# Low parts of the mLSTM query and key weights and tiles on VectorE instead of GpSimd, in a two-layer encoder on one core

## The chip, the cores and the metric

One core of a Trainium2 chip runs the whole program. The metric is the device time of one execution in microseconds. TensorE (PE in the rows) multiplies, VectorE (DVE) and ScalarE (ACT) do the element-wise work, GpSimd (POOL) does some of it, and SyncE (SP) issues most of the loads from HBM.

## The reference

Two encoder layers of 512 tokens and 1024 channels. Each has a token mixer and a channel mixer. The mixer runs two branches on one modulated input u: a bidirectional mLSTM with four heads of 256 channels, and a dilated attention with three patterns. What the change touches are the mLSTM's query and key:

```python
qk = silu(centred_dwconv(u @ w_in[:, :2048], conv_w, conv_b))   # five taps along the tokens
q, k = split(qk, 2)                # 4 heads of 256 channels each
# per head, both directions:
s   = einsum('thd,shd->ts', q, k) * exp(log_d - m)
num = s @ v
h   = num / max(|den|, exp(-m))
y_a = (sigmoid(o) * norm(h) * gn_w) @ w_a
```

Everything is float32.

## The kernel before

**Products in three parts.** Each float32 operand is split in a high part (ScalarE casts it to fp32r, L87) and a low part (operand minus high part, L88, `split`). `mm3` (L90 to L93) issues three matmuls for one product: high by high (L91), then for `product` high weights by the low part of u (L92), then the low weights by the high part of u (L93). So TensorE asks for a tile's low weights only with the third matmul. `split` takes the engine of the subtraction as an argument; VectorE is the default.

**Weights.** `w_feature` (L116 on) loads 256 columns of weights (1 MB) through SP into one of two raw buffers, and gives them out in two halves of 128x1024, each with its high and low part in one of two pairs of buffers. A pair is free again when the product that read it two halves ago is done. The name `wqk` stands in `POOL`, so for query and key weights the subtraction runs on GpSimd; all other weights have it on VectorE.

**A head.** `head_qk` (L1068 to L1087) runs twice for a head, for query and for key, with two halves each: four products of 24 matmuls of 512 columns. Behind each product ScalarE copies the PSUM tile into `zp` (L1077) and makes the first tap (L1079), VectorE adds four taps (L1081, `cy`), ScalarE takes the tanh (L1082), VectorE finishes SiLU (L1083), ScalarE casts the high part `qkh` (L87), and the low part `qkl` is a subtraction of 128x512 (L1085, L88). `GQ = (0, 1)` holds both values of `n % 2`, so all of these run on GpSimd. `zp` and `cy` have two buffers.

After the four products `head_v` (L1089 on) makes the values: its first two PSUM tiles (`mv`) are the same two buffers that the query and key products use (tag `g`), so it can't begin before ScalarE has copied the third and fourth product into `zp`. `head_o` makes the output gate.

**Order.** The heads run in a pipeline: `head_scores` of one head (products `smx`, exponentials `dt`, and the split `pt`), then `weave` alternates the four products, values and gate of the next head with `head_out` of this one (`num`, the denominators `dn` in L1187 to L1201 with one power on GpSimd in L1200, `htp`). The first head's query runs inside the last attention step. Outside blocks under manual schedule, the framework's planner sets each engine's order from its own estimates; each engine then runs its list in order. In the first layer, accumulations of the next modulation (`acc`, L283) run on VectorE between all this, with their loads (`aw`) in SP's queue.

Of the kernel before, what the change touches and what calls it, by code (L numbers as in the profile page):

```python
# [35 lines left out]
NM = 8  # L36
AV = 'gS'
GORD = (0, 1, 2)
GQ = (0, 1)
MV = 'gA'  # L40
SD = ((0, 0, 0.5, 1, 1.5, 3, 3.5, 4, 4.5, 5, 5), (1, 1.5, 2, 2, 2.5, 4, 5.5, 6, 6.5, 7, 7))
SF = ((0, 0, 0.5, 1, 2, 3, 3), (1.5, 2.5, 3.5, 4, 5, 6, 6))
# [5 lines left out]
ENG = {mybir.EngineType.PE, mybir.EngineType.DVE, mybir.EngineType.Activation, mybir.EngineType.Pool}  # L48
OW = ((0, 2), (1, 0), (1, 2))
BG = 1  # L50
POOL = ("wqk",)
WV = (1, 1)
HO = ((0, 0), (0, 1), (1, 0), (0, 2), (1, 1), (0, 3), (1, 2), (1, 3))
Q = 18
# [11 lines left out]
def encoder(ctx: ExitStack, tc: tile.TileContext, a, depth):  # L66
    nc = tc.nc
    alpha = 4 ** 0.25
    V, S, G, Y = nc.vector, nc.scalar, nc.gpsimd, nc.sync
# [13 lines left out]
    def raw_tile(name):  # L83
        return wpool.tile([P, 2048], F32, tag="raw", name=name, bufs=RAW)

    def split(hi, lo, src, eng=None):
        S.copy(hi, src)  # L87
        (eng or V).tensor_tensor(lo, src, hi.bitcast(F32), op=ALU.subtract)  # L88
# [24 lines left out]
    def w_pair(name, off, k, n):  # L113

        return [wpool.tile([P, 1024 + WPAD], F32R, tag=t, name=name + t[1])[:, off:off + k * n]
                .rearrange("p (k n) -> p k n", n=n) for t in ("wh", "wl")]  # L116

    def w_feature(src, ktiles, name, own=None, count=2, eng=None):


        n = src.shape[1]
        cols = 2048 // ktiles
        srcv = src.rearrange("(k p) n -> p k n", p=P)
        for c0 in range(0, n, cols):
            cw = min(cols, n - c0)
            raw = raw_tile(name)
            rv = raw[:, :ktiles * cw].rearrange("p (k n) -> p k n", k=ktiles)
            Y.dma_start(rv, srcv[:, :, c0:c0 + cw])
            for j in range(cw // P):
                r = rv[:, :, j * P:(j + 1) * P]  # L130
                if own is not None and c0 // P + j < count:
                    yield split_own(r, ktiles, own, eng)
                    continue
                wh, wl = w_pair(name, 0, ktiles, P)
                split(wh, wl, r, G if name in POOL else V)
                yield [wh[:, k, :] for k in range(ktiles)], [wl[:, k, :] for k in range(ktiles)]

    def split_own(r, ktiles, own, eng):

        out = [], []  # L140
        for k in range(0, ktiles, 4):
            wh, wl = own(), own()
            split(wh[:], wl[:], r[:, k:k + 4, :], eng)
            for o, w in zip(out, (wh, wl)):
                o.extend(w[:, i, :] for i in range(4))
        return out
# [497 lines left out]
    with ExitStack() as st:  # L644
# [76 lines left out]
        with tc.manual_schedule(engines=ENG):  # L721
            for f in range(KT):
                wh, wl, _ = wq
# [11 lines left out]
    for l in range(depth):  # L735
# [13 lines left out]
        def slot(name, dt=F32):  # L749
            return X.tile([P, T], dt, tag="q", name=name, bufs=Q)  # L750
# [5 lines left out]
        def wk(name, shape=(P, T)):  # L756
            r = roles[name]
            return YP.tile(list(shape), F32, tag=r, name=name, bufs=depths[r])
# [57 lines left out]
        def att_qk(sp, given=None):  # L816

            q, k = {}, {}
            for g in GORD:
                c0 = COL_A + g * 512 + sp * P  # L820
                if given and given[g]:
                    ps = given[g]
                else:
                    ps = yield from gemm_steps(next(w_feature(w_in[:, c0:c0 + P], KT, "waq")), uk, KT, "aq")
                src = ps[:].rearrange("p (a i r) -> p a r i", a=4, r=4)
                if g:
                    q[g] = slot(f"q{g}")
                    S.activation(q[g][:].rearrange("p (a r i) -> p a r i", a=4, r=4), src, AF.Copy,
                                 scale=qsc[:, sp:sp + 1])
                    continue  # L830

                t = slot("q0")
                S.activation(t[:].rearrange("p (a r i) -> p a r i", a=4, r=4), src, AF.Copy, scale=qsc[:, sp:sp + 1])
                q[0] = [YP.tile([P, T + d], F32R, tag=n, name="qs", bufs=2) for n, d in (("cy", 0), ("zp", 4))]
                for s in range(2):
                    own, oth = slice(64 * s, 64 * s + 64), slice(64 - 64 * s, 128 - 64 * s)
                    S.copy(q[0][s][own, 0:T], t[own, :])
                    V.tensor_tensor(q[0][s][oth, 0:T], t[own, :], q[0][s][own, 0:T].bitcast(F32), op=ALU.subtract)
            for g in GORD:
                c0 = COL_A + 1536 + g * 512 + sp * P  # L840
                if given and given[3 + g]:
                    ps = given[3 + g]
                else:
                    w = first_k.pop(g, None) if given else None
                    ps = yield from gemm_steps(w or next(w_feature(w_in[:, c0:c0 + P], KT, "wak")), uk, KT, "ak")
                if g:
                    k[g] = slot(f"k{g}")
                    S.copy(k[g][:].rearrange("p (r j) -> p r j", r=4), ps[:].rearrange("p (j r) -> p r j", r=4))
                    continue

                kk = [slot(f"kk{s}", F32R) for s in range(2)]
                kl = YP.tile([P, T], F32R, tag="xd", name="kl", bufs=XD_)
                for s in range(2):
                    own, oth = slice(64 * s, 64 * s + 64), slice(64 - 64 * s, 128 - 64 * s)
                    S.copy(kk[s][own, :], ps[own, :])
                    S.copy(kk[s][oth, :], ps[own, :])
                    V.tensor_tensor(kl[own, :], ps[own, :], kk[s][own, :].bitcast(F32), op=ALU.subtract)
                k[0] = kk, kl
# [203 lines left out]
        def product(w, name, fine):  # L1062

            if fine:
                return (yield from gemm_steps(w, uk, KT, name))
            return gemm_f(w, uk, KT, name)

        def head_qk(h, sec, out, fine=False):  # L1068

            src = w_in[:, sec * COL_K + h * 256:sec * COL_K + h * 256 + 256]  # L1070
            for d, w in enumerate(w_feature(src, KT, "wqk")):
                n = sec * 8 + 2 * h + d
                ps = yield from product(w, "qk", fine)
                zp = wk("zp", (P, T + 4))
                G.memset(zp[:, 0:2], 0.0)
                G.memset(zp[:, T + 2:T + 4], 0.0)
                S.copy(zp[:, 2:T + 2], ps[:])  # L1077
                y = wk("cy")
                S.activation(y[:], zp[:, 0:T], AF.Identity, bias=vec["convb"](n), scale=vec["conv"](0, n))  # L1079
                for j in range(1, 5):  # L1080
                    V.scalar_tensor_tensor(y[:], zp[:, j:j + T], vec["conv"](j, n), y[:], op0=ALU.mult, op1=ALU.add)  # L1081
                S.activation(zp[:, 0:T], y[:], AF.Tanh, scale=0.5)  # L1082
                V.scalar_tensor_tensor(y[:], zp[:, 0:T], 1.0, y[:], op0=ALU.add, op1=ALU.mult)  # L1083
                th, tl = slot("qkh", F32R), slot("qkl", F32R)
                split(th[:], tl[:], y[:], G if n % 2 in GQ else V)  # L1085
                out.append((th, tl))
                yield  # L1087

# [31 lines left out]
        def head_lead(out):  # L1120

            o, qk = [], []
            yield from head_o(0, o, True)
            yield from head_qk(0, 0, qk, True)
            out.extend((o[0], qk))

        def head_gemm(h, out, begun=()):

            so, qk = begun or ([], [])
            vs, o = [], [so]  # L1130
            if not begun:
                yield from head_qk(h, 0, qk)
            yield from head_qk(h, 1, qk)
            yield from head_v(h, vs)
            if not begun:
                o = []
                yield from head_o(h, o)
            out.extend((qk, *vs, o[0]))
# [127 lines left out]
        for h in range(MH):  # L1266
            for d in range(2):
                th, tl = (PW.tile([P, T], F32R, tag="hgw", name=n, bufs=16) for n in ("hgh", "hgl"))
# [7 lines left out]
        for i in range(KT):  # L1276
# [6 lines left out]
            th = Z.tile([P, T], F32R, name=f"mh{i}")  # L1283
            tl = Z.tile([P, T], F32R, name=f"ml{i}")
# [35 lines left out]
        for i in range(FT):  # L1320
# [17 lines left out]
            th, tl = (F.tile([P, T], F32R, tag="f", name=n, bufs=2 * FT) for n in ("fh", "fl"))  # L1338
# [90 lines left out]
```

## Time and profile before

| what | before |
|---|---|
| time, median of three runs | 2257.79 us (2257.42 to 2259.61) |
| the profiled execution's own time | 2259.71 us |
| span of the profiled execution | 2257.9 us |
| busy: PE, DVE, ACT, POOL | 97%, 58%, 39%, 10% |
| heads of the first layer | about 325 to 570 us of the span |
| heads of the second layer | about 1430 to 1680 us of the span |

The profile is read in this order: the busy shares, then the same by stretch, then what TensorE waited for in the stretches that the change touches, then the groups of instructions there, and last the order of time inside one head. A matmul's row shows its pipelined duration, so consecutive matmuls overlap; idle time and its releaser stand in brackets.

### The profile page before, as it was taken

What the parts mean: (1) busy time and instruction counts of PE and PEld (TensorE: products, weight loads), DVE (VectorE), ACT (ScalarE), POOL (GpSimd) and SP (SyncE); (2) the same over time, 40 slices, a digit from 0 to 9 for tenths busy, and PEclk for the clock granted to TensorE, in tenths of its full rate; (3) what the DMA queues carried; (4) which work ended last, traced back from release to release, by engine and by line L of the source; (5) the groups of instructions that cost most, each with busy time, mean ns of one, the idle gap of its engine ahead of it and who ended that gap; (6) DMA issues with size and microseconds to landing.
All of it is one profiled execution on the core that took longest, in us unless ns stands there. A gap on an engine that the chain in (4) does not pass through costs nothing.

```text
span 2257.9 us, 30948 instructions
## 1 busy us (share of the span) xinstructions
PE 2189.0 (97%) x12353; PEld 1831.3 (81%) x12353; DVE 1307.3 (58%) x2290; ACT 883.7 (39%) x1465; POOL 220.0 (10%) x270
## 2 busy tenths in 40 slices
PE   6999999989999999999999999999999999999998
PEld 5877877878888888888888787788888888888886
DVE  8645348778664766664564544577764455533346
ACT  4544345544333522222364443455543334222222
POOL 4100003322000000000000000233300000000001
PEclk8999999999999999999999999999999999999999
DMA  9623223232343566654543233121212344422324
GB/s 242 188 84 108 85 80 103 75 102 81 106 146 105 196 211 200 202 193 165 184 162 103 62 97 101 57 68 64 75 57 93 103 171 147 163 93 94 112 102 158
DMA packets 244063, 278.78 MB, mean 123 GB/s; under 512 B 10280, under 2 KB 191184, under 8 KB 243920
## 3 DMA queue, kind: packets, MB, share of 16 engines
q1 hardware_dynamic: 238848, 258.97, 35.6%
q0 software_dynamic: 3584, 12.58, 1.6%
q10 hardware_dynamic: 1488, 5.26, 0.6%
q8 instruction: 97, 1.59, 0.3%
q14 instruction: 46, 0.38, 0.1%
HBM read 264.18 MB, written 12.60 MB: 123 GB/s over the span
## 4 chain that ended last, share of the span: by engine, by line
PE 76%; DVE 13%; DMA 4%; ACT 3%; issue 2%; POOL 1%; POOLq 0%; DVEq 0%; SPq 0%; ACTq 0%
PE z L92 6%; PE z L91 6%; PE z L93 6%; DVE cy L1081 5%; DMA aw<-in_w_ada 2%; PE aq L91 2%; PE ak L91 2%; PE aq L93 2%; PE aq L92 2%; PE ak L93 2%; PE ak L92 2%; PE f1y L92 2%; PE f1y L93 2%; PE f1y L91 2%; DVE acc L677 2%
## 5 line engine op out<-in xcount | busy, mean ns | idle before, releaser
L283 DVE SCALAR_TENSOR_TENSOR acc<-aw,cact,acc 128x512 f32<-128x512 f32 x140 | 110.1, 786 | 45.9 <-DMA aw<-in_w_ada 43.8
L1081 DVE SCALAR_TENSOR_TENSOR cy<-zp,vcols,cy 128x512 f32<-128x512 f32 x128 | 115.6, 903 | 10.4 <-ACT cy L1079 8.5
L87 ACT CAST w3h<-w 128x1024 fp32r<-128x1024 f32 x40 | 42.1, 1054 | 151.6 <-PE z L92 147.0
L978 ACT ACTIVATE xs<-xs,sm 128x512 f32<-128x512 f32 x64 | 46.3, 723 | 134.3 <-DVE sm L977 130.6
L87 ACT CAST w1h<-w 128x1024 fp32r<-128x1024 f32 x40 | 42.0, 1050 | 144.3 <-PE z L92 144.3
L88 POOL TENSOR_TENSOR wqkl<-wqk,wqkh 128x1024 fp32r<-128x1024 f32 x32 | 78.0, 2437 | 160.6 <-ACT wqkh L87 158.6
L88 DVE TENSOR_TENSOR w1l<-w,w1h 128x1024 fp32r<-128x1024 f32 x40 | 49.0, 1224 | 76.5 <-ACT w1h L87 76.5
L1337 DVE TENSOR_TENSOR sl<-sl,z 128x512 f32<-128x512 f32 x44 | 30.2, 687 | 100.1 <-PE z L93 96.4
L976 DVE CUSTOM_DVE_ANT_0 xs<-sc,bias 128x512 f32<-128x512 f32 x64 | 43.9, 691 | 75.9 <-PE sc L970 64.9
L91 PE MATMUL z<-um0h,w1h 128*128 128x512 f32 x160 | 62.9, 393 | 0.0
L91 PE MATMUL z<-um0h,w3h 128*128 128x512 f32 x160 | 62.8, 392 | 0.0
L91 PE MATMUL z<-um1h,w3h 128*128 128x512 f32 x160 | 62.5, 391 | 0.0
L93 PE MATMUL z<-um0h,w1l 128*128 128x512 f32 x160 | 62.5, 391 | 0.0
L92 PE MATMUL z<-um0l,w3h 128*128 128x512 f32 x160 | 62.4, 390 | 0.0
L91 PE MATMUL z<-um1h,w1h 128*128 128x512 f32 x160 | 62.4, 390 | 0.0
L93 PE MATMUL z<-um0h,w3l 128*128 128x512 f32 x160 | 62.4, 390 | 0.0
L93 PE MATMUL z<-um1h,w3l 128*128 128x512 f32 x160 | 62.4, 390 | 0.0
L92 PE MATMUL z<-um1l,w1h 128*128 128x512 f32 x160 | 62.3, 390 | 0.0
L92 PE MATMUL z<-um0l,w1h 128*128 128x512 f32 x160 | 62.3, 390 | 0.0
L93 PE MATMUL z<-um1h,w1l 128*128 128x512 f32 x160 | 62.3, 390 | 0.0
L92 PE MATMUL z<-um1l,w3h 128*128 128x512 f32 x160 | 62.3, 390 | 0.0
L87 ACT CAST wqkh<-wqk 128x1024 fp32r<-128x1024 f32 x32 | 33.6, 1049 | 47.8 <-PE o L92 37.4
(544 smaller groups left out, 7140.6 us busy)
## 6 DMA issues: line engine op xcount, KB each, us to landing
w<-in_w SPq DMA_DIRECT2D x44, 1024.0 KB
aw<-in_w_ada SPq DMA_DIRECT2D x160, 256.0 KB
wqk<-in_w_in SPq DMA_DIRECT2D x16, 1024.0 KB
wav<-in_w_in SPq DMA_DIRECT2D x12, 1024.0 KB
wak<-in_w_in SPq DMA_DIRECT2D x20, 512.0 KB
f0v<-in_w SPq DMA_DIRECT2D x10, 1024.0 KB
f1v<-in_w SPq DMA_DIRECT2D x10, 1024.0 KB
waq<-in_w_in SPq DMA_DIRECT2D x18, 512.0 KB
```

The source lines that it names most:

```text
L87: S.copy(hi, src)
L88: (eng or V).tensor_tensor(lo, src, hi.bitcast(F32), op=ALU.subtract)
L91: mm(out, lh, rh, start=first, stop=False)
L92: mm(out, lh, rl, start=False, stop=False)
L93: mm(out, ll, rh, start=False, stop=last)
L283: V.scalar_tensor_tensor(acc[:], raws[k][:], c, acc[:], op0=ALU.mult, op1=ALU.add)
L677: V.scalar_tensor_tensor(s, w, c, s, op0=ALU.mult, op1=ALU.add)
L976: V.tensor_tensor_reduce(x[:], sc[:], bias_tile(ti), 1.0, -3e38, ALU.add, ALU.max, sm[:, 0:1])
L978: S.activation(x[:], x[:], AF.Exp, bias=sm[:, 1:2], scale=ch, accum_out=sm[:, 2:3])
L1081: V.scalar_tensor_tensor(y[:], zp[:, j:j + T], vec["conv"](j, n), y[:], op0=ALU.mult, op1=ALU.add)
L1337: V.tensor_tensor(t[:], t[:], p3[:], op=ALU.mult)
```

## The change

`split` for the weights named `wqk` and for the query and key tiles `qkh`/`qkl` no longer gets GpSimd as its engine, so both subtractions take the default, VectorE. The two constants that chose the engine are gone. Nothing else is edited. GpSimd keeps its small operations: the memsets of the borders of `zp` (L1075, L1076) and the power of a 128x1 column (L1200).

```diff
-GQ = (0, 1)
...
-POOL = ("wqk",)
...
                 wh, wl = w_pair(name, 0, ktiles, P)
-                split(wh, wl, r, G if name in POOL else V)
+                split(wh, wl, r)
                 yield [wh[:, k, :] for k in range(ktiles)], [wl[:, k, :] for k in range(ktiles)]
...
                 th, tl = slot("qkh", F32R), slot("qkl", F32R)
-                split(th[:], tl[:], y[:], G if n % 2 in GQ else V)
+                split(th[:], tl[:], y[:])
                 out.append((th, tl))
```

## Rows read from the trace of the kernel before

**Rows 1.** The page: busy time and share of the span of each engine.

```profile
PE 2189.0 (97%) x12353; PEld 1831.3 (81%) x12353; DVE 1307.3 (58%) x2290; ACT 883.7 (39%) x1465; POOL 220.0 (10%) x270
```

**Rows 2.** Stretches: start:end, length, busy PE, PEld, DVE, ACT, POOL; clock, DMA, GB/s.

```profile
325.00:570.00 245.00, 231.55 (x1370) 198.12 (x1369) 187.95 (x385) 121.52 (x228) 70.46 (x83) 0.99 0.28 91
1430.00:1680.00 250.00, 241.21 (x1421) 205.98 (x1420) 178.51 (x370) 128.81 (x244) 69.61 (x83) 0.99 0.19 64
1619.50:1642.50 23.00, 21.63 (x117) 18.57 (x116) 20.80 (x39) 10.38 (x17) 8.82 (x10) 1.00 0.14 46
1473.60:1477.10 3.50, 3.50 (x17) 3.50 (x18) 3.03 (x4) 1.32 (x2) 1.47 (x3) 0.51 0.74 229
```

**Rows 3.** TensorE's waits, 310 to 560: us in total, times, longest.

```profile
PE mv L92 <- DVE wvl L88: 5.9, 3, 3.0
PE mv L91 <- ACT zp L1077: 3.6, 3, 1.4
PE adaps L293 <- ACT ht L1193: 1.1, 1, 1.1
```

**Rows 4.** The same, 1420 to 1690.

```profile
PE mv L91 <- ACT zp L1077: 7.1, 5, 2.6
```

**Rows 5.** Groups by shape, 310 to 585: busy us, mean ns | idle before, releaser.

```profile
L88 POOL TENSOR_TENSOR wqkl<-wqk,wqkh 128x1024 fp32r<-128x1024 f32 x16 | 39.2, 2450 | 79.7 <-ACT wqkh L87 78.7 <-PE smx L92 0.6
L88 DVE TENSOR_TENSOR wvl<-wv,wvh 128x1024 fp32r<-128x1024 f32 x8 | 9.7, 1216 | 0.0
L88 DVE TENSOR_TENSOR pt<-dt,pt 128x512 fp32r<-128x512 f32 x8 | 5.5, 691 | 1.5 <-ACT pt L87 1.5
L1081 DVE SCALAR_TENSOR_TENSOR cy<-zp,vcols,cy 128x512 f32<-128x512 f32 x64 | 57.0, 891 | 3.1 <-ACT cy L1079 2.2
L1189 DVE TENSOR_TENSOR dn<-dn,gcols 128x1 f32<-128x1 f32 x26 | 9.3, 370 | 0.3
L1201 DVE TENSOR_SCALAR ht<-ht,dn 128x256 f32<-128x256 f32 x13 | 9.3, 719 | 7.3 <-POOL dn L1200 7.3
L283 DVE SCALAR_TENSOR_TENSOR acc<-aw,cact,acc 128x512 f32<-128x512 f32 x21 | 20.9, 994 | 2.4 <-DMA aw<-in_w_ada 2.3
```

**Rows 6.** The same, 1420 to 1690.

```profile
L1081 DVE SCALAR_TENSOR_TENSOR cy<-zp,vcols,cy 128x512 f32<-128x512 f32 x64 | 58.6, 915 | 7.4 <-ACT cy L1079 6.3
L1189 DVE TENSOR_TENSOR dn<-dn,gcols 128x1 f32<-128x1 f32 x26 | 12.0, 478 | 0.4
L1201 DVE TENSOR_SCALAR ht<-ht,dn 128x256 f32<-128x256 f32 x13 | 8.3, 636 | 7.1 <-POOL dn L1200 7.1
```

**Rows 7.** Single lines, 310 to 570: times, ns least/median/most, first and last start.

```profile
L1081 DVE SCALAR_TENSOR_TENSOR cy<-zp,vcols,cy x64: 730/751/2694, 340.2 to 542.8; 128x512 f32<-128x512 f32 x64
L1189 DVE TENSOR_TENSOR dn<-dn,gcols x24: 145/158/2231, 388.5 to 551.9; 128x1 f32<-128x1 f32 x24
L1201 DVE TENSOR_SCALAR ht<-ht,dn x12: 411/412/1507, 396.2 to 554.8; 128x256 f32<-128x256 f32 x12
```

**Rows 8.** Timeline in one head: start us, us, engine, line, operation [idle before <-releaser].

```profile
1619.84 1.65 DVE L1081 SCALAR_TENSOR_TENSOR cy<-zp,vcols,cy 128x512 f32<-128x512 f32 x1
...
1626.72 0.90 DVE L1189 TENSOR_TENSOR dn<-dn,gcols 128x1 f32<-128x1 f32 x1
...
1627.91 2.23 DVE L1189 TENSOR_TENSOR dn<-dn,gcols 128x1 f32<-128x1 f32 x1
```

**Rows 9.** Timeline of GpSimd, then of TensorE, in the same head.

```profile
1627.74 2.40 POOL L88 TENSOR_TENSOR wqkl<-wqk,wqkh 128x1024 fp32r<-128x1024 f32 x1
...
1632.62 0.40 PE L93 MATMUL qk<-uf0h,wqkl 128*128 128x512 f32 x1
...
1642.39 0.39 PE L91 MATMUL mv<-wvh,uf0h 128*128 128x256 f32 x1 [1.37 <-ACT zp L1077]
```

**Rows 10.** Timeline of VectorE, the first head of the second layer.

```profile
1449.40 4.34 DVE L1081 SCALAR_TENSOR_TENSOR cy<-zp,vcols,cy 128x512 f32<-128x512 f32 x3 [0.29 <-ACT cy L1079]
...
1459.02 4.70 DVE L1081 SCALAR_TENSOR_TENSOR cy<-zp,vcols,cy 128x512 f32<-128x512 f32 x4 [2.83 <-ACT cy L1079]
```

## The prediction

> **What bounds the kernel now.** I read the page first: TensorE is busy 97% of the span [rows 1], so an edit elsewhere can only give back, or add to, TensorE's idle time and its slow-clock time. The same view cut to the two stretches with mLSTM heads shows how little that is: TensorE idles 245.0 - 231.6 = 13.4 us in the first layer's and 250.0 - 241.2 = 8.8 us in the second's [rows 2]. Next come the waits behind that idle time. In the first layer they are mostly the values' product waiting for its own low weights (5.9 us), or for the copy of the fourth query/key product out of PSUM (3.6 us); in the second layer almost only the latter, 7.1 us in five waits [rows 3, 4]. Both releasers stand behind VectorE: the low weights are in its queue, and the copy is behind the four taps of the third tile. So VectorE's order in the heads sets the end, though it is busy only 188 of 245 and 179 of 250 us there [rows 2]. In the 23 us of a head in which the four tiles are made it is at 20.8 of 23 [rows 2]. That stretch decides.
>
> [...]
>
> **What the change adds to VectorE.** Thirty-two weight halves and thirty-two tiles, sixteen of each in a layer. The same operation on VectorE stands in the profile: 128x1024 from float32 to fp32r takes 1.22 us (`wvl`), 128x512 takes 0.69 us (`pt`) [rows 5]. That is 16 x 1.22 + 16 x 0.69 = 30.5 us a layer, 61 us in all. GpSimd takes 2.45 us for the former [rows 5], so a low part is also made sooner, if VectorE is free.
>
> **What it gives back.** VectorE pays for GpSimd's work already. One tap of 128x512 has a median of 0.751 us and a longest of 2.69; an operation on a single column of 128x1 has a median of 0.158 us and a longest of 2.23 [rows 7]. In the timeline the 2.23 us one starts 0.17 us after a `wqkl` of 2.40 us begins on GpSimd and ends with it (1630.14) [rows 8, 9]. So these are operations held while GpSimd works. Taking the median as the undisturbed time, the first layer gets back 57.0 - 64 x 0.751 = 8.9 us in the taps, 9.3 - 26 x 0.158 = 5.2 in L1189, 9.3 - 13 x 0.412 = 3.9 in L1201 and, with the tap's median, 20.9 - 21 x 0.751 = 5.1 in `acc`: 23.1 us [rows 5, 7]. The second gets 10.5 + 7.9 + 2.9 = 21.3 us [rows 6, 7]. Net VectorE gains 61.0 - 44.4 = 16.6 us, about 2 us per head, against 57 + 71 us in which it idles in these stretches.
>
> [...] If the stretched rows had another cause, nothing would come back and the sum below would be the second rival's.
>
> **What that does on the path.** Where the work falls matters more than its sum. Take the steady head of the second layer [rows 8, 9]. Of its four `wqkl`, two fall into the gate product and the scores before, where VectorE has room; the third runs before the first tap; one (1627.74) lies in the stretch. Of the four `qkl` two lie before the wait at 1642.39. Added to the chain: 1.22 + 2 x 0.69 = 2.60 us. Returned in the same stretch: 1.65 - 0.75, 0.90 - 0.16 and 2.23 - 0.16 = 3.71 us [rows 8]. The taps of the second and third tile, and so the copy that TensorE waits for, come 1.1 us earlier; the wait is 1.37 us [rows 9], so 1.1 us of it goes. Five heads have this form (two of the first layer, three of the second): 5.5 us.
>
> The other head of the first layer waits 3.0 us for `wvl`, with `acc` also stretched in front: I take 1.5 us of it. In the second layer's first head the wait is 2.6 us [rows 4]; seven taps take 4.34 + 4.70 us where seven medians make 5.26 [rows 7, 10], so 3.8 us comes back against two `wqkl` and two `qkl`, 3.8 us; but a good half of these fall into gaps like the 2.83 us before 1459.02 [rows 10]. I take 1.5 us. For the first layer's first head, of the same form but with `acc` in between, 1.3 us. The wait of `adaps` (1.1 us) is behind a `dn` chain held 0.9 us: 0.9. Together 5.5 + 1.5 + 1.5 + 1.3 + 0.9 = 10.7 us. The slow clock I leave at nothing in the forecast, and at up to 2 x 1.7 us in the range.
>
> **What it costs anew.** A `wqkl` now stands in VectorE's list, behind whatever waits there, in the first layer also behind an `acc` that waits for its load. Behind it stand taps and the `dn` chain, and for those ScalarE's copies and TensorE. The trace has no such wait of the query and key products. The nearest rows are the values' low weights, already on VectorE: 5.9 us for eight halves in the first layer, none for `wvl` among the second's waits [rows 3, 5]. For sixteen halves a layer that makes 0 to 11.8 us. I take 3.4 us, near the lower end, because the fourth half has room: its GpSimd version starts at 1627.74 and TensorE reads it at 1632.62 [rows 9], 4.9 us for an operation of 1.22. Raw buffers are held until the low part is made, so SP's next load starts with it; 1.2 us less work frees them no later unless the queue is that late, and I cost this at nothing. The scores' stretch gets one `wqkl`; VectorE has gaps there. GpSimd's own small operations lose their queue, a gain I count at nothing because the power's column waits for VectorE.
>
> The sum against the profiled execution's own 2259.71 us (1.8 us beyond its span) is 2259.7 - 10.7 + 3.4 = 2252.4 us. That execution lies 1.9 us above the median of the runs, so the forecast is 2250.5 us.
>
> **The rivals.** *No change that can be measured.* The wait moves rather than shrinks: ScalarE works in order, its copy stands behind its tanh and the casts, and the planner, whose order will change with VectorE's load, may place `qkl` and `wqkl` ahead of the taps. Then the 3.7 us returned and the 2.6 added cancel, and 0 to 4 us is left: about 2256 us. For it: the net on VectorE is positive over the whole stage. Against it: the added work is spread, the returned work lies on the chain.
>
> *VectorE becomes the bound.* In the dense stretch it has 23.0 - 20.8 = 2.2 us idle [rows 2]. If the stretch keeps its 20.8 us, because the holds are not GpSimd's or other operations meet them, then 2.60 us of new work per head lengthens the chain by up to that much, and the fourth half's 4.9 us of room is used up when taps and a `dn` chain stand before it. It decides from a queue of 3.7 us ahead of a `wqkl` (4.9 - 1.2). The price is one wait of about 2 us (5.9 / 3) in each of eight heads, 16 us, with half of the 10.7 us still returned: 2257.8 + 16 - 5.4 = 2268 us; with the wait only in the first layer's four heads, 2260 us. [...]
>
> **How the numbers follow.** The forecast (faster, 2243 to 2253) gets 0.53, no change 0.27, VectorE as the bound 0.20. A measurement of this kernel tells about 0.2%, 4.5 us, from no change. The lower end is the forecast without new waits (3.4), with both slow-clock places gone (3.4) and a little more of the 22 us of idle time: 2241. The upper end goes to the middle of the slow rival, 2264. The likeliest case alone spans 2243 to 2253.
>
> **What would show it.** Right, if after the change L1081 has a mean near 0.75 us and L1189 one near 0.16, VectorE's busy time in the heads rises by about 8 us a layer, and the wait of `mv` for `zp` shrinks from 1.4 us to a few tenths. The new cost shows as a wait of `qk` L93 for `wqkl` on VectorE. Wrong, if the taps stay at 0.9 us, or if the waits of `mv` stay while the taps are fast: then the order, not the hold, sets them.

## The result and the profile after the change

The changed kernel takes 2235.15 us (median of four runs, 2232.11 to 2236.06) against 2257.61 us: a ratio of 0.9897, interval 0.9885 to 0.9909. That is 22.5 us, three times the 7.3 us that were forecast, and below the range. The two profiled executions differ by 2259.71 - 2235.07 = 24.6 us; the following shows where. Line numbers of the changed kernel are lower by two: the taps are L1079 there, the `dn` maximum L1187.

The page's busy times answer to [rows 1]. TensorE does the same 12353 matmuls; GpSimd falls from 220 to 94 us; VectorE, with 64 more instructions, hardly moves.

```profile
PE 2181.5 (98%) x12353; PEld 1825.9 (82%) x12353; DVE 1310.6 (59%) x2354; ACT 885.2 (40%) x1465; POOL 94.0 (4%) x206
```

TensorE's waits in the heads, first those of the first layer, then of the second (us in total, times, longest). They answer to [rows 3, 4].

```profile
PE mv L90 <- DVE wvl L86: 1.4, 2, 1.1
PE tp L986 <- DVE xs L978: 1.0, 1, 1.0
PE num L89 <- DVE vl L1104: 0.3, 1, 0.3
...
PE tp L986 <- DVE xs L978: 1.0, 1, 1.0
PE mv L89 <- ACT zp L1075: 0.5, 1, 0.5
PE Amx L1142 <- DVE vl L1104: 0.2, 1, 0.2
PE mv L90 <- DVE wvl L86: 0.2, 1, 0.2
```

Before, the first layer's list had two more lines than those shown in [rows 3], and the second layer's three more:

```profile
PE num L91 <- DVE vl L1106: 2.8, 3, 1.8
PE tp L988 <- DVE xs L980: 1.0, 1, 1.0
...
PE num L91 <- DVE vl L1106: 1.5, 3, 0.5
PE tp L988 <- DVE xs L980: 1.0, 1, 1.0
PE mv L91 <- ACT wvh L87: 0.2, 1, 0.2
```

So the waits went from 14.4 to 2.7 us and from 9.8 to 1.9 us: 19.6 us. No line has the query and key product waiting for `wqkl`. The 1.0 us of `tp` belongs to the attention and is the same in both.

The clock is the next part. The kernel before has three places between its start (the first 110 us) and its last microseconds where the clock is at half, two in the heads and a third one in the second layer's output norm; the changed kernel has none. The place in the second layer's heads stands in [rows 2]; here are the one in the first layer's heads, the third place before, and the third place's 14 matmuls after (start:end, length, busy of PE, PEld, DVE, ACT, POOL, granted clock, DMA share, GB/s):

```profile
367.70:371.20 3.50, 3.50 (x19) 3.50 (x18) 3.46 (x5) 0.74 (x2) 1.17 (x1) 0.51 0.83 284
...
1869.60:1873.10 3.50, 3.50 (x14) 3.02 (x12) 3.17 (x7) 2.90 (x8) 0.11 (x1) 0.51 0.03 10
...
1846.36:1848.26 1.90, 1.90 (x14) 1.68 (x12) 1.86 (x4) 1.51 (x4) 0.00 (x0) 1.00 0.02 6
```

So the third place cost 1.6 us, 3.50 against 1.90 for the same matmuls. The two places in the heads, 3.5 us at 0.51 each, cost some 1.7 us each (3.5 x 0.49, an estimate). They stood behind waits of 2.7 and 2.6 us that are gone. A long wait isn't always followed by one, though: none stood behind the longest wait before, 3.0 us. The third place stood behind a wait of 2.0 us that the changed kernel has, too, so it isn't shown to be the change's.

From the first gate product of a layer's first head to the first product behind its last, the first layer's heads got 258.56 - 244.55 = 14.0 us shorter and the second's 252.29 - 241.62 = 10.7 us (the rows stand under "What comes back"). That is the whole difference. Outside the heads the third place's 1.6 us are offset, above all by 1.3 us more between the two layers' heads. Of the 24.7 us in the heads, 11.5 + 7.8 = 19.4 us are TensorE's idle time, in keeping with the waits, and some 3.4 us the two slow places at 1.7 us each. The last 1.9 us, busy time of TensorE for the same products, I have not traced.

The groups of the second layer's heads, busy us, mean ns | idle before; they answer to [rows 6]:

```profile
L1079 DVE SCALAR_TENSOR_TENSOR cy<-zp,vcols,cy 128x512 f32<-128x512 f32 x64 | 48.0, 750 | 2.6 <-ACT cy L1077 1.5
L86 DVE TENSOR_TENSOR wqkl<-wqk,wqkh 128x1024 fp32r<-128x1024 f32 x16 | 19.5, 1221 | 3.6 <-ACT wqkh L85 3.6
L86 DVE TENSOR_TENSOR qkl<-cy,qkh 128x512 fp32r<-128x512 f32 x16 | 11.0, 688 | 1.4 <-ACT qkh L85 1.4
L1199 DVE TENSOR_SCALAR ht<-ht,dn 128x256 f32<-128x256 f32 x13 | 5.4, 414 | 8.9 <-POOL dn L1198 8.9
L1187 DVE TENSOR_TENSOR dn<-dn,gcols 128x1 f32<-128x1 f32 x26 | 3.5, 155 | 0.2
```

The mean of each formerly stretched group is now the median of before: 750 ns for the taps (915), 155 for the `dn` maximum (478), 414 for L1199 (636).

### The profile page after: what moved, and what is told of

The parts are those of the page before. It is cut to its first block, busy times and chain, and to the rows that moved or that the text cites. A ratio compares the mean times of both kernels' runs of the same rounds, so it can differ in the third digit from the quotient of the medians.

```text
span 2233.2 us, 30962 instructions
## 1 busy us (share of the span) xinstructions
PE 2181.5 (98%) x12353; PEld 1825.9 (82%) x12353; DVE 1310.6 (59%) x2354; ACT 885.2 (40%) x1465; POOL 94.0 (4%) x206
## 4 chain that ended last, share of the span: by engine, by line
PE 84%; DVE 8%; DMA 4%; ACT 2%; issue 1%; POOL 0%; POOLq 0%; DVEq 0%; SPq 0%; ACTq 0%
PE z L90 6%; PE z L89 6%; PE z L91 6%; DMA aw<-in_w_ada 3%; PE qk L89 2%; PE qk L90 2%; PE qk L91 2%; PE aq L89 2%; PE ak L89 2%; PE f1y L90 2%; PE f1y L89 2%; PE f1y L91 2%; PE ak L91 2%; PE ak L90 2%; PE aq L91 2%; PE aq L90 2%
## 5 line engine op out<-in xcount | busy, mean ns | idle before, releaser
L281 DVE SCALAR_TENSOR_TENSOR acc<-aw,cact,acc 128x512 f32<-128x512 f32 x140 | 104.9, 749 | 47.9 <-DMA aw<-in_w_ada 46.2
L1079 DVE SCALAR_TENSOR_TENSOR cy<-zp,vcols,cy 128x512 f32<-128x512 f32 x128 | 95.7, 749 | 4.0 <-ACT cy L1077 2.3
L89 PE MATMUL qk<-u0h,wqkh 128*128 128x512 f32 x128 | 51.1, 399 | 0.0
L89 PE MATMUL qk<-uf0h,wqkh 128*128 128x512 f32 x128 | 50.9, 398 | 0.0
```

The costliest lines, as they stand in the source:

```text
L89: mm(out, lh, rh, start=first, stop=False)
L281: V.scalar_tensor_tensor(acc[:], raws[k][:], c, acc[:], op0=ALU.mult, op1=ALU.add)
```

## The experiments

Three theories were put against each other. **H**: GpSimd's large operations hold VectorE, and lifting the hold is the gain. **O**: the move changed the planner's order of VectorE's work, and that is the gain. **L**: the low parts are made sooner. O is a real rival: in each layer's heads only 319 of VectorE's other instructions, 404 in the first and 374 in the second, stand in a common order before and after.

### The hold taken away, nothing moved

From the kernel before:

```diff
-                split(wh, wl, r, G if name in POOL else V)
+                (S.copy(wh, r), G.memset(wl.bitcast(F32), 0.0)) if name in POOL else split(wh, wl, r)
...
-                split(th[:], tl[:], y[:], G if n % 2 in GQ else V)
+                S.copy(th[:], y[:]); G.memset(tl[:].bitcast(F32), 0.0)
```

> The kernel before, with GpSimd filling the 64 low parts of query and key weights and tiles with zeros instead of subtracting: the low parts are left out, GpSimd still writes the same buffers at the same places, VectorE gets no added work, and the order of TensorE is that of the kernel before. Theory H: without a read on GpSimd nothing is held, so the gain comes without the move: 2230 to 2237 us. Theory O: the order is that of before, so 2255 to 2259 us. Theory L: the fills don't wait for the high parts, so the low parts are early too: 2233 to 2238 us, as with H; the first three runs tell H from L.

Measured: 2233.52 us, ratio 0.9881 (0.9866 to 0.9895). This kernel leaves the low parts out. In the heads of both layers VectorE's order is that of the kernel before but for one exchange of neighbours in each. The order of before, with GpSimd as the engine and no work added to VectorE, gives the whole gain as soon as GpSimd fills instead of subtracting. O falls. L doesn't, because the fills don't wait for the high parts.

### The hold put back, nothing else

Two kernels from the changed one. Each lets GpSimd work, behind each of the 64 subtractions, in the buffer that was just read. The first subtracts:

```diff
-                split(wh, wl, r)
+                split(wh, wl, r); name == "wqk" and G.tensor_tensor(r, r, wh.bitcast(F32), op=ALU.subtract)
...
-                split(th[:], tl[:], y[:])
+                split(th[:], tl[:], y[:]); G.tensor_tensor(y[:], y[:], th[:].bitcast(F32), op=ALU.subtract)
```

> The changed kernel, and behind each of the 64 subtractions on VectorE GpSimd makes the same subtraction again, into the buffer it reads from, which nobody reads afterwards. Nothing of the result depends on it. Theory H: the taps and the 128x1 operations are held again, in a list that now also has the 61 us of subtractions, so most of the gain or more is lost: 2250 to 2270 us, taps at 0.85 us or more. Theories O and L: VectorE's order and the time of the low parts are those of the changed kernel, so 2233 to 2238 us.

The second fills twice:

```diff
-                split(wh, wl, r)
+                split(wh, wl, r); name == "wqk" and [G.memset(r, 0.0) for _ in range(2)]
...
-                split(th[:], tl[:], y[:])
+                split(th[:], tl[:], y[:]); [G.memset(y[:], 0.0) for _ in range(2)]
```

> The changed kernel, and behind each of the 64 subtractions GpSimd fills the same buffer with zeros twice instead of subtracting: work of GpSimd that writes SBUF and reads nothing. [...] If any large GpSimd operation holds VectorE, or if its queue alone (the power of L1200 behind it) costs the time: 2245 us or more.

Measured: 2303.21 us with the subtraction, ratio 1.0186 (1.0171 to 1.0202); 2235.35 us with the fills, ratio 0.9892 (0.9874 to 0.9910). In the second layer's heads the 374 instructions of VectorE besides the moved ones come in the same order in both and in the changed kernel; the low parts are made at the same point of the list. So O falls again and L with it: 68 us lie between subtracting and filling alone, and the fills are 10 us under the 2245 us that a hold by any large operation was to give. GpSimd is busy with either: 79 + 46 us of subtraction, 62 + 34 us of filling. The groups over the whole kernel, of the subtraction:

```profile
L1079 DVE SCALAR_TENSOR_TENSOR cy<-zp,vcols,cy 128x512 f32<-128x512 f32 x128 | 135.8, 1062 | 3.7 <-ACT cy L1077 2.3
L133 POOL TENSOR_TENSOR wqk<-wqk,wqkh 128x1024 f32<-128x1024 f32 x32 | 79.2, 2474 | 187.4 <-DVE wqkl L86 109.7 <-DVE dn L1185 53.6 <-DVE sm L977 18.3
```

and of the fills:

```profile
L1079 DVE SCALAR_TENSOR_TENSOR cy<-zp,vcols,cy 128x512 f32<-128x512 f32 x128 | 95.6, 748 | 4.0 <-ACT cy L1077 2.3
L133 POOL MEMSET wqk<- 128x1024 f32 x64 | 61.5, 961 | 179.0 <-DVE wqkl L86 168.4 <-DVE dn L1185 9.0
```

The taps are stretched to 1062 ns by the one and not at all by the other. The expectation for the subtraction was too low at 2270. Its page has

```profile
PE 2210.7 (96%) x12353; PEld 1848.0 (80%) x12353; DVE 1377.5 (60%) x2354; ACT 883.6 (38%) x1465; POOL 218.7 (10%) x270
```

in a span of 2302.3 us. So against the changed kernel (2181.5 of 2233.2 us) TensorE is idle 40 us more and busy 29 us more for the same matmuls. The mean granted clock was 0.980 against 0.993 in the changed kernel: over the two spans that loses some 30 us more (2302 x 0.020 - 2233 x 0.007, an estimate), about that busy time. Nearly half of the 68 us is thus clock, which the expectation left out; whether a hold itself costs more where VectorE has more to do isn't shown.

### The two halves of the change

From the kernel before, the weights alone and the tiles alone:

```diff
-POOL = ("wqk",)
+POOL = ()
```

> The kernel before with one half of the change: the 32 low parts of the query and key weights (128x1024) come from VectorE, the 32 low parts of the tiles (128x512) stay on GpSimd. Theory H (GpSimd's large operations hold VectorE, and lifting the hold is the gain): the stretch that goes with the weights returns, the tiles' stretch stays, so about 60% of the 22 us: 2242 to 2247 us. Theory O (the planner's new order of VectorE's work is the gain, the holds are not): no bound from the rows, but the taps keep a mean near 0.9 us while the time falls. Theory L (the low weights are made sooner, 1.22 instead of 2.45 us, and that is the gain): nearly all of the gain, 2235 to 2238 us.

```diff
-GQ = (0, 1)
+GQ = ()
```

> The kernel before with the other half of the change: the 32 low parts of the tiles (128x512) come from VectorE, those of the weights (128x1024) stay on GpSimd. By the holds: the weights' holds stay, so some 40% of the gain, 2245 to 2250 us, with taps near 0.82 us. If the two halves add up, this gain and that of the weights alone make the 22 us of both. If held time beyond a head's slack is what costs, the two together give more than the sum or less, by how much each alone stays above the slack: then this one lies outside 2243 to 2252 us.

Measured: 2246.11 us, ratio 0.9937 (0.9919 to 0.9956), and 2253.05 us, ratio 0.9976 (0.9967 to 0.9986). By their ratios the halves give 14 and 5.4 us, together 20 of the 23 that the whole gives by its own; the rest is within the intervals. The weights' result lies where H put it and above what L allows. The tiles gave less than expected (2245 to 2250) though their taps came near what was expected (831 ns): beside GpSimd operations of 2.4 us the waits of `mv` for `zp` stayed, 9.4 us in all (10.7 before).

### What VectorE's added work costs

From the changed kernel, each subtraction twice:

```diff
-                split(wh, wl, r)
+                split(wh, wl, r); name == "wqk" and V.tensor_tensor(wl, r, wh.bitcast(F32), op=ALU.subtract)
...
-                split(th[:], tl[:], y[:])
+                split(th[:], tl[:], y[:]); V.tensor_tensor(tl[:], y[:], th[:].bitcast(F32), op=ALU.subtract)
```

> The changed kernel with each of the 64 subtractions on VectorE made twice: another 61 us of work for VectorE, at the places of the first, and nothing on GpSimd. If the added work lies in gaps of VectorE (why the gain came out double): 2235 to 2242 us. If the work added by the change costs nearly what it takes in the dense stretch of a head (2.6 us per head, as the prediction put it): 2250 to 2260 us, with waits of TensorE for zp or for low weights.

Measured: 2241.90 us, ratio 0.9931 (0.9916 to 0.9945): at the upper end of what gaps allow. The first 61 us of subtractions cost about 2 us (2235.15 against 2233.52 without them, a difference within the intervals), the second 61 us cost 7 us.

### The same hold elsewhere

With the heads free, the changed kernel still holds VectorE in its first 110 us, where accumulations of 128x256 meet GpSimd's low parts of the first weights and of u and take 893 ns on average, against 478 with both of these moved. From the changed kernel, the weights' part to VectorE (two places):

```diff
-        split(wq[0][:], wq[1][:], wq[2], G)
+        split(wq[0][:], wq[1][:], wq[2])
```

> The changed kernel, and the low parts of the eight weight tiles of 128x768 at the kernel's start come from VectorE instead of GpSimd, too. In the first 110 us accumulations of 128x256 are held 11 us in seven places by these, and TensorE waits 8.6 us for the accumulations. By the holds: VectorE gets 8 x 0.95 = 7.6 us and gives back 11 us, so 1 to 4 us less than the changed kernel, 2231 to 2234 us. If DMA sets the start, no change: 2235 us.

Then also u's:

```diff
-            G.tensor_tensor(u[1][:, f, :], ut[:], u[0][:, f, :].bitcast(F32), op=ALU.subtract)
+            V.tensor_tensor(u[1][:, f, :], ut[:], u[0][:, f, :].bitcast(F32), op=ALU.subtract)
```

> The same, and the eight low parts of u (128x512) at the start too. By the holds another 8.9 us come back for 8 x 0.69 = 5.5 us of work: 2229 to 2234 us. Against it: VectorE's order there is by hand, and each of these subtractions waits for two passes of ScalarE (0.8 us each) with the next accumulations queued behind it; if that wait decides, it is slower than with the weights alone, by up to 8 x 1.6 = 13 us.

And with u's issued in the middle of the next tile's accumulations:

```diff
+                if low and k == 4:
+                    low()
...
-            G.tensor_tensor(u[1][:, f, :], ut[:], u[0][:, f, :].bitcast(F32), op=ALU.subtract)
+            return lambda: V.tensor_tensor(u[1][:, f, :], ut[:], u[0][:, f, :].bitcast(F32), op=ALU.subtract)
...
-                    acc = mod_acc(raws)
+                    acc = mod_acc(raws, low)
...
-                        modulate(f + 1, acc)
+                        low = modulate(f + 1, acc)
```

> As the start with all low parts on VectorE, but each of the eight low parts of u is issued by hand in the middle of the next tile's accumulations, so that VectorE no longer waits for ScalarE's two passes. If the 10.1 us that VectorE waited for ScalarE were what made that kernel slower than the one with the weights alone: the holds that remain there, 48 x (0.631 - 0.478) = 7.3 us, come back for 5.5 us of work, and it gives 2220 to 2224 us. If something else of the move made it slower, 2227 to 2231 us as before.

Measured: 2224.19 us (0.9853, 0.9837 to 0.9870), 2229.15 us (0.9874, 0.9859 to 0.9889) and 2219.81 us (0.9818, 0.9800 to 0.9836). The first gains more than expected, so DMA alone doesn't set the start. The second takes the last holds away and is slower than the first: VectorE now waits 10.1 us for ScalarE, with accumulations behind. The third takes most of that wait away and keeps the gain; it is the fastest version here. Not all of these differences come from holds: in the first 110 us the clock was 0.89 in the changed kernel and 0.98, 0.92 and 0.98 in these three, while TensorE waited 8.6 us for accumulations in the changed kernel and 3.4, 7.7 and 3.0 us in these. The expectations left the clock out. Group, busy us, mean ns, in the first 110 us: the changed kernel, weights moved, both moved, both moved and issued late.

```profile
L675 DVE SCALAR_TENSOR_TENSOR acc<-araw,cact,acc 128x256 f32<-128x256 f32 x48 | 39.7, 893 | 0.0
```

```profile
L675 DVE SCALAR_TENSOR_TENSOR acc<-araw,cact,acc 128x256 f32<-128x256 f32 x48 | 27.2, 631 | 0.0
```

```profile
L675 DVE SCALAR_TENSOR_TENSOR acc<-araw,cact,acc 128x256 f32<-128x256 f32 x48 | 19.9, 478 | 0.0
L690 DVE TENSOR_TENSOR u0l<-ut,u0h 128x512 fp32r<-128x512 f32 x8 | 5.5, 691 | 10.1 <-ACT ut L689 10.1
```

```profile
L677 DVE SCALAR_TENSOR_TENSOR acc<-araw,cact,acc 128x256 f32<-128x256 f32 x48 | 20.3, 479 | 0.0
L692 DVE TENSOR_TENSOR u0l<-ut,u0h 128x512 fp32r<-128x512 f32 x8 | 5.5, 693 | 3.7 <-ACT ut L691 3.7
```

## Why the prediction was right or wrong

**The bound: right.** The gain is TensorE's idle time in the heads, 19.4 of 24.7 us, and the slow clock there, some 3.4 us; 1.9 us are not traced.

**The mechanism: right.** The stretched rows were held by GpSimd's subtractions; the fills and the idle subtractions show it (taps of 748 ns and 1062 ns on average), and the means went to the medians as named beforehand. What in a subtraction holds them, its reads or another part of it, is not shown.

**What is added: right.** 1.22 and 0.69 us were taken, 1.221 and 0.688 us measured.

**What comes back: right in size.** I counted the excess of three or four groups over their medians, 44.4 us, and forecast some 8 us more of VectorE's time per layer. From the first gate product of a layer's first head to the first product behind its last, VectorE's busy time was (before, after, then with zeros for the low parts; columns as in the stretches above):

```profile
307.78:566.34 258.56, 244.15 (x1477) 207.21 (x1474) 192.62 (x405) 125.69 (x234) 72.84 (x84) 0.99 0.27 88
1417.40:1669.69 252.29, 242.53 (x1464) 206.22 (x1461) 177.04 (x375) 126.67 (x236) 72.00 (x84) 0.99 0.20 66
```

```profile
307.47:552.02 244.55, 241.66 (x1478) 205.90 (x1474) 192.47 (x437) 126.82 (x234) 10.13 (x52) 1.00 0.29 93
1404.38:1646.00 241.62, 239.69 (x1464) 204.66 (x1461) 179.97 (x407) 126.94 (x236) 9.44 (x52) 1.00 0.21 69
```

```profile
309.15:552.55 243.40, 241.60 (x1477) 206.03 (x1474) 171.72 (x405) 126.66 (x234) 33.19 (x84) 1.00 0.29 94
1403.31:1644.20 240.89, 239.33 (x1465) 204.46 (x1462) 157.82 (x375) 126.76 (x236) 33.20 (x84) 1.00 0.21 69
```

Busy time fell by 0.2 us in the first layer and rose by 2.9 us in the second. But where neighbouring rows overlap it counts the time once, so it is not the sum by which I had forecast. Added up row by row, VectorE's times in these stretches are 211.8 and 192.8 us before, 216.9 and 199.9 us after: 5.1 and 7.1 us more. Against the 30.5 us that were added to each, 25.5 and 23.4 us came back, 48.9 us in all. With zeros, where nothing is added, the busy time fell by 20.9 and 19.2 us, 40.1 us in all.

**The path: the step that failed.** "Added to the chain: 1.22 + 2 x 0.69 = 2.60 us" left a net gain of 1.1 us per steady head. Measured in that head, the added work took 0.6 us of the chain and the net was 2.3 us. The chain is VectorE's from the first tap of the first tile to the end of the third tile's taps. Its first row before is the tap at 1619.84 of [rows 8]; the others follow, before, with zeros for the low parts (nothing added, and the order of before), and after.

```profile
1637.69 3.45 DVE L1081 SCALAR_TENSOR_TENSOR cy<-zp,vcols,cy 128x512 f32<-128x512 f32 x4 [0.62 <-ACT cy L1079]
```

```profile
1596.54 0.75 DVE L1081 SCALAR_TENSOR_TENSOR cy<-zp,vcols,cy 128x512 f32<-128x512 f32 x1
...
1611.82 3.12 DVE L1081 SCALAR_TENSOR_TENSOR cy<-zp,vcols,cy 128x512 f32<-128x512 f32 x4 [0.62 <-ACT cy L1079]
```

```profile
1598.34 0.75 DVE L1079 SCALAR_TENSOR_TENSOR cy<-zp,vcols,cy 128x512 f32<-128x512 f32 x1
...
1614.21 3.10 DVE L1079 SCALAR_TENSOR_TENSOR cy<-zp,vcols,cy 128x512 f32<-128x512 f32 x4
```

That is 21.30, 18.40 and 18.97 us. Without the holds 2.9 us came back, where I had 3.71; with the moved work, and the order that came with it, 0.57 us was added, where I had 2.60. TensorE's side is the stretch from the head's first `mv` matmul to its first `o` matmul, where both its waits lie, before and after:

```profile
1639.44 0.28 PE L91 MATMUL mv<-wvh,uf0h 128*128 128x256 f32 x1
...
1655.05 0.39 PE L91 MATMUL o<-uf0h,woh 128*128 128x512 f32 x1
```

```profile
1617.93 0.28 PE L89 MATMUL mv<-wvh,uf0h 128*128 128x256 f32 x1
...
1631.44 0.40 PE L89 MATMUL o<-uf0h,woh 128*128 128x512 f32 x1
```

15.61 us and 13.51: the gain is 2.1 us, the whole of what TensorE loses there. Why the moved work added so little stands in VectorE's timeline after:

```profile
1604.17 0.69 DVE L86 TENSOR_TENSOR qkl<-cy,qkh 128x512 fp32r<-128x512 f32 x1
...
1605.03 1.21 DVE L86 TENSOR_TENSOR wqkl<-wqk,wqkh 128x1024 fp32r<-128x1024 f32 x1
1606.17 0.15 DVE L1187 TENSOR_TENSOR dn<-dn,gcols 128x1 f32<-128x1 f32 x1
1606.24 0.15 DVE L1185 TENSOR_SCALAR dn<-num 128x1 f32<-128x1 f32 x1
1606.31 0.74 DVE L1079 SCALAR_TENSOR_TENSOR cy<-zp,vcols,cy 128x512 f32<-128x512 f32 x1
```

The first tile's `qkl` and the fourth half's `wqkl` run while the second tile's first tap still waits for ScalarE's first pass, whose row after and before are these, the latter with the tap behind it:

```profile
1605.08 0.81 ACT L1077 ACTIVATE cy<-zp,vcols 128x512 f32<-128x512 f32 x1
```

```profile
1627.56 0.82 ACT L1079 ACTIVATE cy<-zp,vcols 128x512 f32<-128x512 f32 x1
...
1630.26 0.73 DVE L1081 SCALAR_TENSOR_TENSOR cy<-zp,vcols,cy 128x512 f32<-128x512 f32 x1
```

After, the tap starts 0.4 us behind the end of the pass (1605.89); before, 1.9 us behind it (1628.38), because the 2.23 us hold [rows 8] stood on that place. The third tile's taps end at 1617.31, 0.6 us before `mv` begins; TensorE then has no wait left to give, in that head or in its `num`. I had treated the whole 23 us stretch as one chain because VectorE was 90% busy in it, but part of that busy time was the hold itself, which is the very thing that was to go.

The waits behind the chain were priced too low as well. In the five steady heads 9.4 us of TensorE's waits went where I had 5.5; in the other three 9.3 us went where I had 4.3, so the shares that I took there were too small. One wait had no term in the sum at all: `num` waiting for `vl`, 4.3 us over all heads, of which 4.0 us went.

**New waits, 3.4 us: none.** The rival with VectorE as the bound has no support: no product waits for `wqkl`. Its price is real but begins later; it took another 61 us of work to see 7 us. VectorE's 20.8 of 23 us, from which that rival reckoned its 2.2 us of room, were in part the holds of the very work that was moved.

**The clock: sized at nothing.** The two slow places in the heads went, and with them some 3.4 us; this stood in the range and not in the sum. No run times the range's 2 x 1.7 us directly; what the trace before shows is two places of 3.5 us at 0.51, and the changed kernel has neither. Together: 10.7 us of waits were expected to go and 19.6 went, 3.4 us of new ones were expected and none came, and 3.4 us of clock were left out.

**No change that can be measured:** it needed the order to set the waits. With the order of before and without the hold TensorE's waits in the heads fall to 1.8 and 1.6 us, so it falls.

## What to carry to other kernels

When VectorE looks full in a stretch, look first at the longest against the median of each of its groups: here an operation on one column, 0.158 us at the median, once took 2.23 us, and GpSimd's timeline showed a subtraction of 2.40 us that ended with it [rows 7, 8, 9]. Work taken back from GpSimd was nearly free here (61 us of it cost about 2 us), because it could run where the hold had been, and a small kernel that lets GpSimd fill instead of subtract tells the hold from the order in one run. Before sizing the gain, list every wait of the engine that bounds the stretch: one of 4.3 us stood in the list here and not in the sum. After such a move, look for the next wait that the moved instruction itself makes in its new list: u's low parts made VectorE wait 10.1 us for ScalarE here.

## What the runs showed of the hardware

One operation was longer beside fills. In the kernel with zeros the `TENSOR_SCALAR` of 128x256 has a median of 414 ns and a longest of 1555. One such row on VectorE, beside fills of 0.52 and 0.95 us, then these on GpSimd:

```profile
1601.81 1.55 DVE L1201 TENSOR_SCALAR ht<-ht,dn 128x256 f32<-128x256 f32 x1 [0.44 <-POOL zp L1075]
```

```profile
1601.76 0.52 POOL L1085 MEMSET qkl<- 128x512 f32 x1
1602.23 0.09 POOL L1076 MEMSET zp<- 128x2 f32 x1
1602.26 0.95 POOL L135 MEMSET wqkl<- 128x1024 f32 x1
```

The taps have a mean of 748 ns in both kernels that fill, and of 1062 ns beside the idle subtractions. So here the taps were held by GpSimd's subtractions and not by its fills, and this operation was longer beside fills, up to 1555 ns in one of the two kernels and up to 585 in the other.

I had not expected how steep the cost of holds is. The same 64 subtractions on GpSimd cost 22 us in the kernel before, and 68 us where VectorE also did its own. Of the 68 us about 30 are the clock, at a mean of 0.980 against 0.993 in the changed kernel (an estimate), and 40 are TensorE's idle time.
